# Rotating 96 images by 90 degrees: the last load in four strided pieces, and the first store gated by the first of them

## The chip, the cores and the metric

The kernel runs on one core of one Trainium2 chip. The metric is device time in microseconds (us) of the whole program, the median of several executions. A profile of one execution goes with it; its times count from the first instruction of the span.

## The reference

The input is 32 x 3 images of 256 x 256 float32 values, and each is turned clockwise by a quarter:

```python
def setup_inputs():
    batch, c, h, w = 32, 3, 256, 256
    return {"x": np.random.randn(batch, c, h, w).astype(np.float32)}

def reference(x: np.ndarray) -> np.ndarray:
    return np.rot90(x, k=-1, axes=(-2, -1)).astype(np.float32)
```

The output value at row r, column c of an image is the input value at row 255 - c, column r. No arithmetic is done. 25.17 MB are read from HBM, 25.17 MB are written.

## The kernel before

The 96 images are cut into 12 slabs of 8 images, 2 MB each. Each slab has an SBUF tile of its own (`units[0]` to `units[11]`, 128 partitions x 2 halves x 2048 values, so 8 KB for each partition and half); there is also one such tile in PSUM, `turned0`. `last` is 11.

**Loads** (lines 61 to 68). All 24 loads, two of 1 MB for each slab, are issued by SyncE (SP) in the order of the slabs. A middle slab (1 to 10) is loaded with 16 rows of an image to a partition: its first half goes to the even partitions, its second half to the odd ones, 64 partitions with 16 KB each (line 66). The first and the last slab are loaded with 8 rows to a partition: half i goes to all 128 partitions, 8 KB each (line 64). One contiguous run is one packet of the DMA, so packets are of 16 KB for the middle slabs and of 8 KB for the other two. `mark` (line 68) remembers the load of the first half of the last slab.

**Turning** (lines 70 to 82). VectorE (DVE) transposes blocks of 32 x 32 values; the access patterns of source and destination put the blocks where the rotation wants them. Each slab takes two instructions. The result of slab n is written into the tile of slab n - 1, which has been read by then; that of slab 0 goes to PSUM.

**Stores** (lines 84 to 97). They are issued by SP too, behind all loads, in packets of 8 KB. Slab 1 is stored first, in two halves of 1 MB (lines 85 and 88). A dependency written out by hand makes the first of these wait until `mark` has landed, "stores after loads". Slabs 2 and 11 are stored in two halves as well (line 91), slabs 3 to 10 with 2 MB each (line 93). Last comes slab 0: ScalarE (ACT) copies each half from PSUM into the tile of the last slab (line 96), free by then, and each half is stored (line 97).

Three things order the work around the change. SP issues its DMAs strictly in the program's order and waits, at each, for all that this DMA depends on; what is behind it waits too. The DMAs' completions are counted on eight semaphores in rotation, so a DMA also waits until the one eight places earlier has landed, which keeps at most eight loads in flight. And all DMAs go through one queue, spread over the 16 DMA engines; each DMA ends with one small completion packet on each engine.

Of the kernel before, what the change touches and what calls it, by code (L numbers as in the profile page):

```python
# [1 line left out]

# [4 lines left out]

@with_exitstack
def kernel(
    ctx: ExitStack,
    tc: tile.TileContext,
    x: bass.AP,
    out: bass.AP,
):

    nc = tc.nc
    fp32 = mybir.dt.float32

    B, C, H, W = x.shape  # L40
    P = nc.NUM_PARTITIONS
    RI, RO = 16, 8
    K = H // RI
    I = 2
    Q = P // (K * I)
    n_slabs = B * C // (Q * I)
    last = n_slabs - 1
    F = RO * W

    rows_in = x.rearrange("b c h w -> (b c h) w")  # L50
    rows_out = out.rearrange("b c h w -> (b c h) w")
    ld8_v = rows_in.rearrange("(n i p r) w -> n p i (r w)", i=I, p=P, r=RO)
    ld16_v = rows_in.rearrange("(n i m r) w -> n i m (r w)", i=I, m=Q * K, r=RI)
    st_v = rows_out.rearrange("(n i p c) w -> n p i (c w)", i=I, p=P, c=RO)

    pools = [ctx.enter_context(tc.tile_pool(name=f"unit{u}", bufs=1)) for u in range(n_slabs)]
    units = [pool.tile([P, I, F], fp32, name=f"u{u}") for u, pool in enumerate(pools)]
    psum = ctx.enter_context(tc.tile_pool(name="psum", bufs=1, space=bass.MemoryType.PSUM))
    turned0 = psum.tile([P, I, F], fp32, name="turned0")

    for n in range(n_slabs):
        for i in range(I):
            if n in (0, last):
                ld = nc.sync.dma_start(out=units[n][:, i], in_=ld8_v[n][:, i])  # L64
            else:
                ld = nc.sync.dma_start(out=units[n][i::I].rearrange("p i f -> p (i f)"), in_=ld16_v[n, i])  # L66
            if (n, i) == (last, 0):
                mark = ld

    for n in range(n_slabs):  # L70
        t_in, t_out = units[n], units[n - 1] if n else turned0
        if n in (0, last):
            for i in range(I):
                src = t_in[:, i].rearrange("p (r g c) -> p c r g", r=RO, c=RO)
                dst = t_out[:, i].rearrange("p (c g r) -> p c r g", c=RO, r=RO)
                nc.vector.transpose(out=dst[:, :, ::-1, ::-1], in_=src)  # L76
        else:
            src = t_in.rearrange("p i f -> p (i f)").rearrange("p (r g c) -> p c r g", r=RI, c=RO)
            dst = t_out.rearrange("p i (c k r) -> p c r k i", c=RO, r=RI)[:, :, ::-1, ::-1, :]
            for h in range(2):  # L80
                cs = slice(h * RO // 2, (h + 1) * RO // 2)
                nc.vector.transpose(out=dst[:, cs], in_=src[:, cs])  # L82

        if n == 1:
            first = nc.sync.dma_start(out=st_v[n][:, 0], in_=t_out[:, 0])  # L85
            tc.add_manual_dep(first.ins, mark.ins.name, mybir.DependencyInfo(
                mybir.DependencyClass.Sync, mybir.DependencyReason.SCHED_ONLY), reason="stores after loads")
            nc.sync.dma_start(out=st_v[n][:, 1], in_=t_out[:, 1])
        elif n in (2, last):
            for i in range(I):  # L90
                nc.sync.dma_start(out=st_v[n][:, i], in_=t_out[:, i])
        elif n:
            nc.sync.dma_start(out=st_v[n], in_=t_out)

    for i in range(I):
        nc.scalar.copy(out=units[last][:, i], in_=turned0[:, i])  # L96
        nc.sync.dma_start(out=st_v[0][:, i], in_=units[last][:, i])


# [1 line left out]
_INS = ['x']  # L101
_OUTS = [((32, 3, 256, 256), 'float32')]


# [23 lines left out]
```

## Time and profile before

| | |
|---|---|
| three runs | 123.69, 124.05, 124.07 us; median 124.05 |
| the profiled execution | 124.07 us, of which the span from first to last instruction is 122.3 |
| DVE busy | 93.3 us (76%), 24 instructions |
| ACT busy | 5.0 us (4%), 3 instructions |
| DMA | 50.33 MB in 5504 packets, mean 412 GB/s over the span |
| packets under 512 B | 640: 40 DMAs x 16 engines, the completions |
| loads | 24 of 1 MB, median 19.6 us from issue to landing |
| stores | 8 of 2 MB, median 22.0 us; 8 of 1 MB, median 13.7 us |

DVE works without a pause from 5.7 us to 99.4 us, one slab in 7.8 us. The stores begin near 60 us, when DVE has turned half of the slabs, and DVE stays ahead of them to the end. A DMA's time from issue to landing is mostly time in the queue behind others. The rows of SP that bear a line number show when it issued a DMA; they say nothing of when the data moved.

### The profile page before, as it was taken

The numbers are of one execution on the slowest core, as the hardware profiler recorded it, in microseconds if no ns is written. First come the engines' busy times: TensorE is split into PE (matmuls) and PEld (weight loads), VectorE is DVE, ScalarE is ACT, GpSimd is POOL, SyncE is SP. The second block draws the span as 40 slices with busy tenths as digits, with TensorE's granted clock in tenths as the row PEclk, the third lists the DMA queues.
The fourth block names the chain that finished last, engine by engine and source line by source line (L and its number), as shares of the span: only waits on it lengthen the run. The fifth ranks groups of instructions, "written<-read, shape, count | busy, mean of one in ns | idle before, by whom it ended". The sixth has DMA issues, their size and how long they took to land.

```text
span 122.3 us, 138 instructions
## 1 busy us (share of the span) xinstructions
DVE 93.3 (76%) x24; ACT 5.0 (4%) x3; POOL 0.2 (0%) x4
## 2 busy tenths in 40 slices
DVE  0199999999999999999999999999999950000000
ACT  0000000000000000000400000000000641000000
POOL 0000000000000000000000000000000000000000
DMA  3999999999999999999999999999999999999994
GB/s 86 426 431 429 434 429 434 439 429 439 423 429 429 429 429 429 429 429 405 423 423 429 429 426 429 429 426 418 423 429 415 418 421 426 426 421 415 418 421 193
DMA packets 5504, 50.33 MB, mean 412 GB/s; under 512 B 640, under 2 KB 640, under 8 KB 640
## 3 DMA queue, kind: packets, MB, share of 16 engines
q1 hardware_dynamic: 5504, 50.33, 97.9%
HBM read 25.17 MB, written 25.17 MB: 412 GB/s over the span
## 4 chain that ended last, share of the span: by engine, by line
DMA 49%; DVE 16%; issue 10%; DVEq 3%; SPq 3%; ACT 2%
DMA u<-in_x_dram 45%; DVE u L82 13%; DMA out_dram<-u 4%; DVE u L76 3%; DVEq L123 3%; SPq L66 2%; ACT u L96 2%; SPq L64 1%; SPq L85 0%
## 5 line engine op out<-in xcount | busy, mean ns | idle before, releaser
L82 DVE STREAM_TRANSPOSE u<-u 128x2048 f32<-128x2048 f32 x20 | 78.0, 3945 | 0.3
L76 DVE STREAM_TRANSPOSE turned<-u 128x2048 f32<-128x2048 f32 x2 | 7.6, 3828 | 5.7 <-DMA u<-in_x_dram 5.7
L76 DVE STREAM_TRANSPOSE u<-u 128x2048 f32<-128x2048 f32 x2 | 7.7, 3953 | 0.0
L96 ACT COPY u<-turned 128x2048 f32<-128x2048 f32 x2 | 3.7, 1866 | 36.6 <-DVE u L76 36.6
L96 ACT ACT_TABLE_LOAD x1 | 1.3, 1283 | 59.6 <-DMA u<-in_x_dram 59.6
L112 POOL MEMSET const-bfloat16-1.0<- 128x1 bf16 x1 | 0.1, 102 | 0.0
L112 POOL MEMSET const-uint8-127<- 128x1 uint8 x1 | 0.1, 101 | 0.0
L112 POOL MEMSET const-float32-0.0<- 128x1 f32 x1 | 0.1, 99 | 0.2 <-issue 0.2
L112 POOL MEMSET const-float32-1.0<- 128x1 f32 x1 | 0.1, 98 | 0.0
## 6 DMA issues: line engine op xcount, KB each, us to landing
u<-in_x_dram SPq DMA_DIRECT2D x24, 1024.0 KB, 19.6
out_dram<-u SPq DMA_DIRECT2D x8, 2048.0 KB, 22.0
out_dram<-u SPq DMA_DIRECT2D x8, 1024.0 KB, 13.7
```

What stands on the lines that cost most here:

```text
L64: ld = nc.sync.dma_start(out=units[n][:, i], in_=ld8_v[n][:, i])
L66: ld = nc.sync.dma_start(out=units[n][i::I].rearrange("p i f -> p (i f)"), in_=ld16_v[n, i])
L76: nc.vector.transpose(out=dst[:, :, ::-1, ::-1], in_=src)
L82: nc.vector.transpose(out=dst[:, cs], in_=src[:, cs])
L96: nc.scalar.copy(out=units[last][:, i], in_=turned0[:, i])
L112: nc = _bacc.Bacc("TRN2", target_bir_lowering=False, num_devices=1)
L123: with _tile.TileContext(nc) as tc:
```

## The change

The load of the second half of the last slab, 1 MB into 128 partitions, is split into four DMAs by partition: every eighth partition from 0 (16 partitions, 128 KB), every eighth from 4 (16), every fourth from 2 (32), and the odd ones (64). They are issued in this order. `mark` is now the first of them, instead of the load of the first half of that slab; the first store waits for it. Slabs 2 and 11 are stored by one DMA of 2 MB each, as the slabs between them, and so is slab 0, after both of ACT's copies. The program has 27 loads and 13 stores where it had 24 and 16. Nothing else is touched; DVE's and ACT's instructions are the same in the same order.

```diff
     for n in range(n_slabs):
         for i in range(I):
-            if n in (0, last):
-                ld = nc.sync.dma_start(out=units[n][:, i], in_=ld8_v[n][:, i])
+            if n == last and i:
+                parts = [slice(0, P, 8), slice(4, P, 8), slice(2, P, 4), slice(1, P, 2)]
+                mark = [nc.sync.dma_start(out=units[n][ps, i], in_=ld8_v[n][ps, i]) for ps in parts][0]
+            elif n in (0, last):
+                nc.sync.dma_start(out=units[n][:, i], in_=ld8_v[n][:, i])
             else:
-                ld = nc.sync.dma_start(out=units[n][i::I].rearrange("p i f -> p (i f)"), in_=ld16_v[n, i])
-            if (n, i) == (last, 0):
-                mark = ld
+                nc.sync.dma_start(out=units[n][i::I].rearrange("p i f -> p (i f)"), in_=ld16_v[n, i])
...
             nc.sync.dma_start(out=st_v[n][:, 1], in_=t_out[:, 1])
-        elif n in (2, last):
-            for i in range(I):
-                nc.sync.dma_start(out=st_v[n][:, i], in_=t_out[:, i])
         elif n:
             nc.sync.dma_start(out=st_v[n], in_=t_out)
 
     for i in range(I):
         nc.scalar.copy(out=units[last][:, i], in_=turned0[:, i])
-        nc.sync.dma_start(out=st_v[0][:, i], in_=units[last][:, i])
+    nc.sync.dma_start(out=st_v[0], in_=units[last])
```

## The prediction

> **What bounds the kernel now.** I read the page's slices first, then the DMA queue, then SP's waits, then the stretch around the change. In the page, the first line is the busy share of the 16 DMA engines in 40 slices of 3.06 us, the second what they moved, the third the queue's share of the span.
>
> ```profile
> DMA  3999999999999999999999999999999999999994
> GB/s 86 426 431 429 434 429 434 439 429 439 423 429 429 429 429 429 429 429 405 423 423 429 429 426 429 429 426 418 423 429 415 418 421 426 426 421 415 418 421 193
> q1 hardware_dynamic: 5504, 50.33, 97.9%
> ```
>
> The DMA engines are full from the second slice to the last but one. No compute engine can be the bound: what counts is how many bytes there are (unchanged), at what rate they move, and whether the stream ever runs dry. The switch from loads to stores lies near 61 us, at the border of slices 19 and 20 (423, 423 GB/s), and shows no hole. A closer look, in windows (stretch, its length, DVE, ACT, POOL busy, clock, DMA share, GB/s):
>
> ```profile
> 40.00:59.50 19.50, 19.43 (x6) 0.00 (x0) 0.00 (x0) 1.00 0.99 422
> 59.50:61.00 1.50, 1.47 (x2) 1.28 (x1) 0.00 (x0) 1.00 1.03 431
> 61.00:62.50 1.50, 1.50 (x1) 0.00 (x0) 0.00 (x0) 1.00 1.02 426
> 62.50:64.00 1.50, 1.50 (x1) 0.00 (x0) 0.00 (x0) 1.00 1.00 421
> 64.00:76.00 12.00, 11.93 (x5) 0.00 (x0) 0.00 (x0) 1.00 1.01 428
> 92.00:108.00 16.00, 7.37 (x2) 3.73 (x2) 0.00 (x0) 1.00 1.01 421
> 108.00:120.50 12.50, 0.00 (x0) 0.00 (x0) 0.00 (x0) 1.00 1.01 420
> ```
>
> The share stays at 1.00 or above through the switch (a packet counts in the window in which it starts, so a short window can pass 1). The present gate therefore loses nothing: no time is to be had there. SP's waits and issues around it (first who waits, us in total, times, longest; then the timeline's start, duration, instruction):
>
> ```profile
> SPq L66 <- DMA u<-in_x_dram: 25.8, 14, 2.0
> SPq L85 <- DMA u<-in_x_dram: 16.8, 1, 16.8
> ```
>
> ```profile
> 59.64 0.35 SPq L85 DMA_DIRECT2D out_dram<-u  x1
> 60.03 0.43 SPq L88 DMA_DIRECT2D out_dram<-u  x1
> 60.56 2.10 SPq L91 DMA_DIRECT2D out_dram<-u  x2
> ```
>
> SP sits 16.8 us at L85 until the first half of the last slab has landed (59.55), then issues the first store at 59.64. Loads go out eight deep and take 19.6 us each from issue to landing: 19.6 / 8 = 2.45 us per 1 MB. The last load, issued at 42.40, so lands at 62.0, and by the trace's packet records its last packets start between 60.9 and 61.2 on the 16 engines and end between 61.2 and 61.5, where store packets follow at once. A packet of 8 KB takes 0.309 to 0.32 us on its engine.
>
> **The change, part by part.**
>
> *The split load.* The last 1 MB load becomes pieces of 16, 16, 32 and 64 partitions, 128, 128, 256 and 512 KB: 1, 1, 2 and 4 packets of 8 KB for each engine, if each piece is spread over all 16. Bytes and packet size stay. Each piece ends with one completion packet per engine; those take 0.007 to 0.009 us in the records. Three more pieces: 3 x 0.009 = 0.03 us on the load side. SP's three more issues (0.33 us for an issue of this line, less or equal for a piece) go out when older loads land, at 42.4, 44.8, 47.3 and 49.7 by the present rhythm, inside SP's wait of 16.8 us and 10 us before the data's turn; without that cover they would cost 3 x 0.33 = 1.0 us.
>
> *The merged stores.* Slabs 2, 11 (last) and 0 go out as 2 MB instead of twice 1 MB. That saves three issues and three completion packets per engine, 0.03 us, which pays for the pieces: 40 DMAs before and after. Late stores of either form move alike by the landing records (4.98 us per 2 MB as one, 2.52 + 2.46 as two), so: 0. The last slab's store now waits for both transposes, 99.4 instead of 95.6, and slab 0's for both copies, 101.3. Today the store issued at 99.4 lands at 116.5, because 17 us of stores stand ahead of it; an unhindered 1 MB lands in 4.9, and the second half adds 2.5. Cover: 17.1 - 4.9 - 2.5 = 9.7 us. Nothing queued behind them on SP but each other and the end. DVE and ACT get a few more semaphore waits at 91.6 and 99.4 (17 to 28 ns each), under the same cover.
>
> *The moved gate, the one part on the path.* The gate opens when the first piece has landed: one packet per engine later, 2.45 / 8 = 0.31 us. The first store is issued at 59.64 + 0.31 = 59.95 instead of 59.64, and the two after it move along (the second is needed 2.45 us after the first, so it has room). What stands in the queue at that time shrinks from 2.45 us of loads to 7/8 of it, 2.14. Everything hangs on whether a store issued at 59.95 still comes in time. I bound it by two rows, DMA from issue to landing, first for the loads of L64, then for the store of L85:
>
> ```profile
> DMA to landing us min/median/max: 4.9/13.3/19.6
> ```
>
> ```profile
> DMA to landing us min/median/max: 4.9/4.9/4.9
> ```
>
> The minimum of the first is the kernel's first load, into empty queues: issued 0.72, landed 5.66 by the landing records, 4.94 us. The store took 59.64 to 64.50, 4.86 us, and landed 2.48 us after the last load: the stream, not its own start, set that time. So the present gate is within 0.1 us of what an unhindered 1 MB transfer needs. The upper bound: if the store needs the same 4.94 us, it lands at 59.95 + 4.94 = 64.89 against 64.50, a hole of **0.39 us**. The lower bound is **0**: the store reads SBUF where the first load read HBM, and its engines are already running, so its first bytes can be quicker by more than 0.39; nothing in the trace shows how much. The first packets of the first load start 1.05 to 1.83 us after its issue, at different times on different engines; the stores would be needed 1.25 to 1.6 us after theirs (61.2 to 61.55 less 59.95). That is the midst of the range, so I take the middle, **0.2 us**. A gain below 0 is excluded for this part, since the stream has no hole there.
>
> The sum: 124.07 (the profiled execution: 122.3 us of span and 1.8 around it) + 0.03 - 0.03 + 0 + 0.2 = 124.27, and, as that execution is 0.02 above the median of 124.05, **124.25 us**.
>
> [...]
>
> **The rivals.**
>
> *A: the full hole.* The store needs the 4.94 us of the first load. For it: the engines get their first descriptors over 0.8 us there, and the stream cannot hide it. Against: the load's HBM read is in it. 124.05 + 0.39 = 124.44. It decides from 4.92 us on (0.37 us of hole).
>
> *B, the one that ends clearly slower: the small pieces run under the full rate.* Place: the last 1 MB of loads. With one packet per piece and engine, in partitions 8 apart, engines could meet at the same part of SBUF, or completions could come too close together (0.31 us, where 2.45 is the closest in the trace). Price: if the first two pieces run at half rate, 2 x 0.31 = 0.62, 124.7; it decides from 0.37 us, the 1 MB taking 2.84 instead of 2.47. Against: the 64-partition loads also go to every second partition and run at 0.611 us per 16 KB, full rate. It would show the same if a piece were not spread over 16 engines, in which case the gate is not an eighth at all. [...]
>
> *C: hidden anyway.* The store starts quickly enough: 124.05.
>
> *D: faster.* Stores run at 428 GB/s from 64 to 76 us and at 420 to 421 after 92; their packets go from 0.309 to 0.314 us. If the other order of stores kept the first rate to the end, the 18.7 MB from 76 us on would take 43.7 instead of 44.4 us: -0.7, 123.35. For it: only that the rate is seen to differ. Against: it fell among 2 MB stores and did not come back with the 1 MB stores at the end.
>
> **How the numbers follow.** A difference under 0.3% (0.37 us) is about what a measurement of this kernel can tell from no change; the three runs lie 0.38 apart. Forecast (hole of 0 to 0.36) 0.53, C 0.07: within 0.3%, 0.60. A 0.15 and B 0.15: slower, 0.30. D 0.10: faster. The likeliest is 124.25. The range: down to 123.6, which leaves out most of D (0.08), up to 124.9, past A and B's price with the scatter of a run, leaving out some 0.05 where B reaches more pieces.
>
> **What would show it.** SP's wait at the first store's line ends at 59.9 and its issue starts near 59.95; the DMA share of 61.0 to 62.5 us falls from 1.02 to about 0.9 (0.2 / 1.5 = 0.13); the first store lands 4.7 to 4.9 us after issue. A landing 4.5 us after issue, with the share still at 1, is C; 4.9 with a hole is A. If the gate opens at 60.2 or later, or the last load lands past 62.2, it is B. A late store rate of 428 GB/s is D. I am wrong in kind if the time moves while the stretch from 59 to 65 us looks as before.

## The result, and the profile after

The changed kernel takes 124.75 us (median of 6 runs, which lie between 124.34 and 124.90), the kernel before 123.91 in the same session: ratio 1.0063, 95% interval 1.0045 to 1.0080. It is slower by 0.84 us, twice what a measurement can tell from no change. The profiled execution took 124.90 us with a span of 123.1, 0.83 above that of before. Each of the two profiles is that of the slowest execution of its six.

What the DMA engines moved in 40 slices (here of 3.08 us):

```profile
DMA  3999999999999999999999999999999999999995
GB/s 125 413 442 426 426 426 426 426 437 437 405 426 426 442 431 453 452 426 389 333 415 426 423 407 426 426 423 410 423 421 410 426 423 413 421 423 418 415 426 216
q1 hardware_dynamic: 5504, 50.33, 98.0%
```

The engines are as busy as before, but the 19th and 20th slices (55.4 to 61.6 us) move 389 and 333 GB/s where they moved 405 and 423. Busy engines that move less: packets take longer (8 KB in mostly 0.46 to 0.53 us in the first two pieces, where the kernel before takes 0.309 to 0.32). The windows around the switch (columns as in the prediction) say where:

```profile
59.50:61.00 1.50, 1.47 (x2) 0.89 (x1) 0.00 (x0) 1.00 0.94 317
61.00:62.50 1.50, 1.50 (x1) 0.39 (x1) 0.00 (x0) 1.00 1.01 421
62.50:64.00 1.50, 1.50 (x1) 0.00 (x0) 0.00 (x0) 1.00 0.97 399
64.00:76.00 12.00, 11.97 (x4) 0.00 (x0) 0.00 (x0) 1.00 1.01 423
92.00:108.00 16.00, 7.53 (x2) 3.73 (x2) 0.00 (x0) 1.00 1.01 420
108.00:120.50 12.50, 0.00 (x0) 0.00 (x0) 0.00 (x0) 1.00 1.01 420
```

Two things differ. From 59.5 to 61.0, before the switch, 317 GB/s move instead of 431: that is the split load. And the stores run at 423 GB/s from 64 to 76 us, where they had 428. SP's wait and issues of the first stores:

```profile
SPq L86 <- DMA u<-in_x_dram: 10.3, 1, 10.3
```

```profile
60.69 0.35 SPq L86 DMA_DIRECT2D out_dram<-u  x1
61.09 0.43 SPq L89 DMA_DIRECT2D out_dram<-u  x1
61.62 2.22 SPq L91 DMA_DIRECT2D out_dram<-u  x2
```

The first store goes out at 60.69, not at 59.95: the gate opened late too. The packet records complete the account. In the first two pieces an 8 KB packet takes mostly 0.46 to 0.53 us, in the third about 0.43 and then 0.35, in the fourth 0.31 again. (The records do not name the DMA or the engine; this is read from their times.) Each piece is spread over all 16 engines: every one has 16 landings, those of the first between 59.44 and 60.59 us. Landings, averaged over the 16 engines: the loads end at 62.29 instead of 61.79 (+0.50), the stores then take 59.80 instead of 59.32 us (+0.48), and the slowest engine is 0.2 behind the mean at the end instead of 0.35 (-0.15). Together +0.83 for this execution. The engines stand idle between loads and stores for 0.04 us on average, so there is hardly a hole.

Part of the gate's lateness belongs to this execution: one load's landing on the first and on the last engine lay 0.80 us apart, 0.39 before, and the gate waited for the last (the first piece's at 60.59, the issue at 60.69). In another kernel with the same gate and the same sets of partitions in SBUF (runs in HBM alone, below) the store went out at 60.34.

### The profile page after: what moved, and what is told of

Read it like the earlier page. It is cut to its first block, busy times and chain, and to the rows that moved or that the text cites. A ratio compares the mean times of both kernels' runs of the same rounds, so it can differ in the third digit from the quotient of the medians.

```text
span 123.1 us, 139 instructions
## 1 busy us (share of the span) xinstructions
DVE 93.5 (76%) x24; ACT 5.0 (4%) x3; POOL 0.2 (0%) x4
## 4 chain that ended last, share of the span: by engine, by line
DVE 46%; issue 27%; DMA 4%; DVEq 3%; ACT 2%
DVE u L83 37%; DVE turned L77 6%; DMA u<-in_x_dram 4%; DVE u L77 3%; DVEq L121 3%; ACT u L94 2%; DVEq L77 0%
```

## The experiments

The working theory after the result: the strided pieces run below the full rate (S), because of where they lie (P) or because they are short (S2). Against it the hole in front of the first store (H) and the merged stores (M). Ratios are to the kernel before, run beside each kernel on the same chip. Lead means the mean landing of the last load less the issue of the first store; the time of the stores runs from that mean landing to the mean end.

**Parts of the change alone.** The split with the old gate and stores:

```diff
+            if n == last and i:
+                parts = [slice(0, P, 8), slice(4, P, 8), slice(2, P, 4), slice(1, P, 2)]
+                for ps in parts:
+                    nc.sync.dma_start(out=units[n][ps, i], in_=ld8_v[n][ps, i])
```

> The last 1 MB load in the four strided pieces of the change; the gate stays at the landing of the slab's first half, and the stores are those of before. Theory S (the pieces themselves run below the full rate, because of which partitions they hold): packets of the first three pieces take 0.35 to 0.5 us instead of 0.31, the loads end 0.5 to 0.6 us later, ratio 1.004 to 1.005. Rival H (the later gate leaves a hole in front of the first store): no hole is made here, ratio 0.999 to 1.001. Rival M (the merged stores are slower): ratio 0.999 to 1.001.

Measured 1.0037 (1.0025 to 1.0049), just under what S expected. Its loads end at 62.28 on average, 0.49 later than before, and its stores then run at the old pace:

```profile
59.50:61.00 1.50, 1.47 (x2) 1.14 (x1) 0.00 (x0) 1.00 1.02 350
61.00:62.50 1.50, 1.50 (x1) 0.15 (x1) 0.00 (x0) 1.00 0.97 404
64.00:76.00 12.00, 11.93 (x5) 0.00 (x0) 0.00 (x0) 1.00 1.01 427
```

350 GB/s in the first window, 427 in the last: the split alone costs the half microsecond of the loads, and nothing after them.

The merge alone (the three pairs of 1 MB stores as 2 MB each):

> Only the stores of slabs 2, 11 and 0 merged into 2 MB each; loads and gate as before. Theory S: nothing, ratio 0.999 to 1.001. Rival M: the store stretch is slower from the start (423 GB/s instead of 428 from 64 to 76 us), ratio 1.001 to 1.003. Rival H: nothing.

Measured 1.0011 (1.0001 to 1.0021), some 0.1 us, at the edge of what can be seen. The ratio lies in M's range, but M's sign is not there: the stores ran at 427 GB/s from 64 to 76 us, and the stretch was 59.27 us. Where the 0.1 us went stays open.

Split and merge, with the old gate:

> The change without its later gate: strided pieces and merged stores, the first store again gated by the slab's first half. If the gate's move costs nothing of its own, this is as slow as the change, ratio 1.005 to 1.007. If the move costs the rest of the sum of the parts (1.0063 less 1.0037 of the split and 1.0011 of the merge), 1.0045 to 1.005.

Measured 1.0042 (1.0026 to 1.0057), so the move of the gate has about 0.002 of the 1.0063, some 0.26 us, by itself, though the two intervals overlap. Its stores took 59.24 us, 0.56 less than those of the change: one profile each puts the gate's share at twice what the ratios do.

**Where the pieces' slowness comes from.** First, pieces cut along the row of each partition, 128 partitions in each:

```diff
-                parts = [slice(0, P, 8), slice(4, P, 8), slice(2, P, 4), slice(1, P, 2)]
-                mark = [nc.sync.dma_start(out=units[n][ps, i], in_=ld8_v[n][ps, i]) for ps in parts][0]
+                parts = [slice(0, F // 8), slice(F // 8, F // 4), slice(F // 4, F // 2), slice(F // 2, F)]
+                mark = [nc.sync.dma_start(out=units[n][:, i, fs], in_=ld8_v[n][:, i, fs]) for fs in parts][0]
```

> The changed kernel with its last 1 MB load cut along the 8 KB of each partition (1, 1, 2 and 4 KB from all 128 partitions) instead of by partitions; gate on the first piece, an eighth again, stores merged, as many pieces and completions as in the changed kernel. Theory S: without the sparse sets of partitions the loads run at the full rate but for the shorter packets of 1 and 2 KB; the gate opens by 60.0 us and the ratio to the kernel before is 1.000 to 1.003. Rival S2 (it is four completions close together that cost, not the partitions): loads end 0.5 us late here too, ratio 1.004 to 1.007. Rival H: the hole stays, up to 0.39 us, ratio up to 1.003 with load packets at full rate.

Measured 1.0117 (1.0090 to 1.0145): a miss for both. The short packets had a trouble of their own: in the first piece some 1 KB packets took up to 0.5 us and engines stood idle (0.2 us on average). What can still be read: the pieces then landed at 61.26, 61.60, 62.24 and 63.49, that is 0.34, 0.64 and 1.25 us for 128, 256 and 512 KB, nearly the full rate with completions 0.34 us apart. Completions that close together did not cost here, which speaks against S2. Each of these pieces has eight packets for each engine, though; whether a piece of one packet for each engine is slow by its shortness alone, wherever it lies, no run tested.

Then the sets of partitions themselves, on either side of the transfer: runs of neighbours in SBUF and in HBM, in HBM alone, in SBUF alone.

```diff
...
-                mark = [nc.sync.dma_start(out=units[n][ps, i], in_=ld8_v[n][ps, i]) for ps in parts][0]
+                strided = [slice(0, P, 8), slice(4, P, 8), slice(2, P, 4), slice(1, P, 2)]
+                runs = [slice(0, 16), slice(16, 32), slice(32, 64), slice(64, P)]
+                mark = [nc.sync.dma_start(out=units[n][ps, i], in_=ld8_v[n][hs, i]) for ps, hs in zip(runs, runs)][0]
```

> The changed kernel with its four pieces cut as runs of neighbouring partitions (0 to 15, 16 to 31, 32 to 63, 64 to 127) instead of strided sets; sizes, count, gate and stores as in the change. Theory P (the strided sets are slow, in HBM or SBUF): full rate, ratio to the kernel before about 1.001 to 1.002. Rival S2 (short pieces with their completions close together are slow, whatever they hold): packets of 0.35 to 0.5 us as in the change, ratio 1.005 to 1.008. Rival Q (16 neighbouring partitions share few ways into SBUF): slower than the change, packets of 0.6 us and more in the first pieces, ratio above 1.008.

> As the change in SBUF (strided sets of partitions), but each piece reads a run of neighbouring 8 KB rows of HBM, so the last 1 MB is put into the wrong partitions and half a slab of the output is permuted. If the HBM side of the strided pieces is slow: full rate, ratio 1.001 to 1.002. If the SBUF side or the shortness of the pieces is: as the change, 1.005 to 1.008.

> The reverse: pieces go to runs of neighbouring partitions but read the strided rows of HBM of the change (the same half slab of the output is permuted in another way). If the HBM side is slow: as the change, 1.005 to 1.008. If the strided SBUF side is: 1.001 to 1.002. If neighbouring partitions share few ways into SBUF: as the kernel with runs on both sides, whatever that is.

| last 1 MB: SBUF side | HBM side | ratio |
|---|---|---|
| strided (the change) | strided | 1.0063 (1.0045 to 1.0080) |
| strided | runs | 1.0057 (1.0042 to 1.0071) |
| runs | strided | 1.0246 (1.0221 to 1.0271) |
| runs | runs | 1.0233 (1.0215 to 1.0251) |

The HBM side makes no difference that can be seen; with the pieces' sizes kept, the SBUF side takes the loss from 0.6% to 2.3% or more. Windows of the kernel before, and below it of the kernel with runs on both sides:

```profile
58.50:61.50 3.00, 2.96 (x2) 1.28 (x1) 0.00 (x0) 1.00 0.99 410
61.50:64.00 2.50, 2.50 (x1) 0.00 (x0) 0.00 (x0) 1.00 1.03 436
66.00:76.00 10.00, 9.93 (x4) 0.00 (x0) 0.00 (x0) 1.00 1.01 428
76.00:92.00 16.00, 15.93 (x5) 0.00 (x0) 0.00 (x0) 1.00 1.01 423
108.00:119.00 11.00, 0.00 (x0) 0.00 (x0) 0.00 (x0) 1.00 1.01 419
```

```profile
58.50:61.50 3.00, 2.96 (x2) 0.47 (x1) 0.00 (x0) 1.00 1.16 183
61.50:64.00 2.50, 2.50 (x1) 0.81 (x1) 0.00 (x0) 1.00 0.93 200
76.00:92.00 16.00, 15.93 (x5) 0.00 (x0) 0.00 (x0) 1.00 1.01 429
108.00:119.00 11.00, 0.00 (x0) 0.00 (x0) 0.00 (x0) 1.00 1.01 427
```

In the first two rows of the latter the engines are busy and move less than half the rate. Packets take up to 1.2 us, mostly 0.9 to 1.2, while the pieces of 16 and 32 neighbours run, and about 0.6 in that of 64. In the change every eighth partition took 0.46 to 0.53, every fourth 0.43 and then 0.35, and the odd ones 0.31. What rival Q expected came (a ratio above 1.008, packets of 0.6 us and more); the few shared ways that it names were the author's conjecture, and no run shows them. Why a set is slow stays open, for the neighbours as for the strided pieces. The runs show that which partitions a piece holds in SBUF decides how much is lost, and how much that is.

The last two rows were not expected: after so slow a load, the stores run at 427 to 429 GB/s to the end, where the kernel before falls to 419.

**What the gate costs.** To see how fast a store starts, the gate was put on the whole last load:

```diff
-            if (n, i) == (last, 0):
+            if (n, i) == (last, 1):
```

> The kernel before with the gate moved to the landing of the whole last load: SP issues the first store near 62.1 us, into empty queues. It measures what a store needs from issue to landing when nothing stands before it, the quantity that the prediction had to bound. By the first load's row, 4.94 us: the first store lands at 67.05 instead of 64.50, ratio 1.0205 (+2.55 us). If the store starts quicker, by 0.4 us say: 4.54, landing at 66.65, ratio 1.017.

Measured 1.0033 (1.0017 to 1.0049). It did not test what it was made for: in the program as built the second store, which had no gate, went first, at 44.9 us, and queued behind the loads; the gated one followed at 62.10. So all stores of slabs 1 to 11 were given the dependency:

> The kernel before with all stores of slabs 1 to 11 held until the whole last load has landed; in the kernel with the gate on the last load alone, SP had issued the second store at 44.9 us, ahead of the gated one, so that no hole could form. Now the first store is issued near 62.1 us into empty queues. It measures what a store needs from issue to landing with nothing before it. By the first load's row, 4.94 us: landing at 67.05 instead of 64.50, ratio 1.0205. If it starts 0.4 us quicker: 66.65, ratio 1.017.

Measured 1.0184 (1.0165 to 1.0203). The first store's issue, and the hole:

```profile
62.17 0.82 SPq L85 DMA_DIRECT2D out_dram<-u  x2
```

```profile
60.50:61.25 0.75, 0.75 (x1) 0.47 (x1) 0.00 (x0) 1.00 0.86 360
61.25:62.00 0.75, 0.75 (x1) 0.00 (x0) 0.00 (x0) 1.00 0.04 11
62.00:62.75 0.75, 0.75 (x1) 0.00 (x0) 0.00 (x0) 1.00 0.00 0
62.75:63.50 0.75, 0.75 (x1) 0.00 (x0) 0.00 (x0) 1.00 0.84 350
66.00:76.00 10.00, 9.93 (x4) 0.00 (x0) 0.00 (x0) 1.00 1.00 410
```

Its first packets start 0.85 to 1.0 us after the issue, on all engines within 0.15 us, and it lands after 3.91 us. The first load into empty queues needs 4.94, with first packets after 1.05 to 1.83 us. So here a store into empty queues had to be issued 0.85 to 1.0 us ahead of its turn, and H is refuted as a hole. Its landing, 1.6 us later than before, is less than the 2.3 us that this kernel loses: the last row shows where most of the rest went, in stores that run at 410 GB/s behind the hole instead of 428.

The gate's move without any split: a GpSimd copy stands between the landing and the store.

```diff
...
+    spare = spare_pool.tile([P, 64], fp32, name="spare")
...
-                mark = ld
+                mark = nc.gpsimd.tensor_copy(out=spare[:, :], in_=units[n][:, i, :64])
```

> The kernel before, loads and stores as they were, but the first store now waits for a GpSimd copy of 64 columns of the slab's first half into a spare tile, which waits for the landing of that half: the store goes out some 0.2 to 0.4 us later than before, near 59.9, with the last load in one piece. With all stores held until the loads had landed, the first packets started 0.85 to 1.0 us after the issue; the loads end at 61.2 to 61.5. Theory (the move of the gate by itself is hidden): no hole, ratio 0.999 to 1.001. Rival H (a store that late leaves a hole): 0.2 to 0.4 us, ratio 1.0015 to 1.003.

> The same with 512 columns: the store goes out some 0.6 to 1.2 us later than before. With 0.85 to 1.0 us from issue to first packets, holes begin when the issue is later than 60.3 and grow one for one: an issue at 60.5 costs 0.1 to 0.3 us (1.001 to 1.002), one at 60.8 0.4 to 0.6 us (1.003 to 1.005). If nothing is lost even there, the start of a queued store is quicker than that of one in empty queues.

With 64 columns the store went out at 59.80 (0.16 later than before): 1.0029 (1.0019 to 1.0039). With 512 columns at 60.21 (0.57 later): 1.0045 (1.0033 to 1.0057). Neither has a hole (engines idle for 0.01 us), and both are slower than a gate whose move is hidden; the first lies in H's range, but without H's hole. In the second, the stores are slow from the start:

```profile
61.50:64.00 2.50, 2.50 (x1) 0.00 (x0) 0.00 (x0) 1.00 1.01 423
66.00:76.00 10.00, 9.93 (x4) 0.00 (x0) 0.00 (x0) 1.00 1.01 417
76.00:92.00 16.00, 15.93 (x5) 0.00 (x0) 0.00 (x0) 1.00 1.01 419
```

417 GB/s from 66 to 76 us, where the kernel before has 428; packets take 0.317 us on average there instead of 0.310. This is the other part of the change's loss, without pieces and without a hole. What the added copy itself may cost was not measured apart; the profiled execution of the first of the two, at 124.02 us, is the fastest of its seven (median 124.28), so its profile shows little of its 0.3%.

Across the kernels, from one profile each:

| kernel | lead, us | stores, us |
|---|---|---|
| pieces along the row | 1.46 | 59.98 |
| late gate, 512 columns | 1.55 | 59.83 |
| the change | 1.60 | 59.80 |
| late gate, 64 columns | 1.98 | 59.43 |
| runs in HBM alone | 1.99 | 59.45 |
| before | 2.15 | 59.32 |
| merge alone | 2.21 | 59.27 |
| split and merge | 2.37 | 59.24 |
| split alone | 2.39 | 59.17 |
| runs in SBUF alone | 2.98 | 58.63 |
| runs on both sides | 3.92 | 58.44 |

In this table, the earlier the stores are queued ahead of the loads' landing, the faster they run. Two kernels are not in it. That with all stores held has a lead of -0.36 and a hole. That with the gate on the last load alone does not fit: its first store had a lead of 17.0 us, the others were issued from 62.10 on, and its stores took 59.42 us. So one early store is not enough. Even so, the table asked for the gate to be moved the other way.

```diff
-            if (n, i) == (last, 0):
+            if (n, i) == (last - 1, 1):
```

> The kernel before with the first store gated one step earlier, by the landing of the last load of slab 10 (near 57.1 us), so that it is issued 4.6 us before the loads have landed instead of 2.2. In the kernels so far the store stretch, from the mean landing of the loads to the mean end, was shorter the earlier the first store had been issued: 59.8 us at a lead of 1.6 us, 59.4 at 2.0, 59.3 at 2.2, 59.2 at 2.4, and 58.4 to 58.6 at 3.0 to 3.9 (the latter with pieces that also pushed the engines apart). Theory L (the lead itself sets the pace of the stores): 58.5, ratio 0.993 to 0.995, faster than both kernels. Theory F (a late issue disturbs how the engines stand to each other, an early enough one changes nothing, and it was the pushing apart that made the store packets take 0.309 us to the end): as the kernel before, ratio 0.999 to 1.001.

Measured 0.9978 (0.9967 to 0.9989): 123.70 us against 124.06 for the kernel before in that session, so faster than that kernel and, by the ratios, than the change.

```profile
58.50:61.50 3.00, 2.96 (x2) 1.28 (x1) 0.00 (x0) 1.00 0.94 374
61.50:64.00 2.50, 2.50 (x1) 0.00 (x0) 0.00 (x0) 1.00 1.04 439
66.00:76.00 10.00, 9.93 (x4) 0.00 (x0) 0.00 (x0) 1.00 1.02 430
76.00:92.00 16.00, 15.93 (x5) 0.00 (x0) 0.00 (x0) 1.00 1.01 427
108.00:119.00 11.00, 0.00 (x0) 0.00 (x0) 0.00 (x0) 1.00 1.01 429
```

The first row pays: with stores already queued, the last loads are disturbed (374 GB/s instead of 410, the DMA share 0.94 instead of 0.99) and end 0.27 us later on average, at 62.06. The other rows gain: store packets take 0.309 us in every stretch to the end, and the stores need 58.75 us, 0.57 less, with a lead of 4.90 us. Net -0.30 in the profiles, about what the ratio says. Theory L had the direction and left out what the loads lose; theory F, that nothing changes, falls. But F's other half is not refuted: at the switch the engines were pushed apart here too (one DMA's landings spread over 0.36 us before and 0.63 to 0.77 after). In the three kernels whose stores kept or nearly kept 0.309 us (this one and the two with runs in SBUF) that spread is 0.6 us or more during the stores; in most of the slow ones it is 0.3 to 0.55. But it is 0.8 to 0.9 in the kernel with pieces along the row, which has the slowest stores of the table, and grows to 1.1 in that with the gate on the last load: a wide spread is not enough either. Whether the lead acts by itself or by the distance it leaves between the engines or by something else stays open: the packet records do not name the engine.

## Why the prediction was right or wrong

The range, 123.6 to 124.9, holds 124.75; the likeliest case does not: it was "within 0.3%" at 124.25, and the change is slower by 0.63%. That the range held is in part luck. Its top was set by rivals A and B; B came, A did not, and a cost that stood in no term and in no rival took A's place. The kernel before was also quicker in that session (123.91) than the 124.05 that the range started from: 124.05 + 0.84 is 124.89.

- **What bounds the kernel** was right: the DMA stream alone (its engines are busy 97.9% of the span before, 98.0% after), and no hole to be closed at the old switch (DMA share 1.03 and 1.02 from 59.5 to 62.5 us).
- **"Bytes and packet size stay"**, taken to mean that the time of a packet stays, is the step that failed. It let the pieces run at 0.309 to 0.32 us a packet; they took 0.46 to 0.53 in the first two. The cost was in the text as rival B, with a guess at the cause (engines meeting at the same part of SBUF, which no run shows) and 0.62 us as its price; the loads ended 0.50 later. Both of B's signs came: the gate opened after 60.2, the last load landed after 62.2 (at 62.83). B had 0.15 of the chance; against it stood that "the 64-partition loads also go to every second partition and run at 0.611 us per 16 KB, full rate". That row does not carry over: it speaks for the fourth piece, the odd partitions, which ran at full rate (0.31 us per 8 KB) just as those loads do, and not for sets of partitions four or eight apart with one or two packets for each engine. Which of the two, the set or the few packets, makes the strided pieces slow was not separated.
- **The hole** of 0.2 us was mis-sized: 0.04 us. The bound of 4.94 us from the first load was too far off: a store into empty queues lands 3.91 us after its issue. Rival A is refuted, and of C the part is right that the start is hidden.
- **The gate's cost** nevertheless came, as the prediction did not foresee: not as idle time but as store packets that are up to 1.4% longer (0.314 us on average instead of 0.310 from 66 to 76 us; 59.80 us for all the stores instead of 59.32). The prediction looked for holes as the only cost of the gate: "A gain below 0 is excluded for this part, since the stream has no hole there". A full stream ran at two paces here (0.309 us a packet to the end with the early gate, 0.317 from 66 to 76 us with the late one of 512 columns); rival D had that, but only as a gain from the order of the stores. The early gate shows that a gain was to be had.
- **The time of the gate**, 59.95, was 60.69: slow pieces, and an execution with its engines further apart. An issue of a piece took SP 0.49 to 0.52 us, not 0.33 or less; inside SP's wait that cost nothing.
- **The merged stores at 0**: 1.0011, small, place unknown.
- **Rival D** had 0.10, with the 428 GB/s not coming back against it. The rate is real: 427 to 430 to the end in two of the kernels. But the order of the stores does not bring it (the merge alone has 419 to 421 after 92 us); moving the gate earlier did, and the change moves it later.

## What to carry to other kernels

When a load is cut by partition, ask which partitions each piece holds: here pieces with one packet for each engine lost about a third of their rate or more (every eighth partition: 0.46 to 0.53 us a packet instead of 0.31) or up to three quarters (16 neighbours: up to 1.2 us), whatever their HBM side (ratios 1.0063 and 1.0057, 1.0246 and 1.0233). A busy DMA row is not a row at full pace (here 317 GB/s at a share of 0.94, where the kernel before had 431 at 1.03): compare GB/s and packet times between stretches, since the loss here was in load packets of 0.46 us and store packets of 0.314 instead of 0.310 and not in gaps. When loads turn into stores on one queue, try the gate of the first stores earlier (here a lead of 4.9 us was better than 2.2, and 1.6 worse) and count what the last loads lose by it.

## What the runs showed of the hardware

- A store into empty queues starts moving 0.85 to 1.0 us after its issue and lands 3.91 us after it (1 MB); the first load of the program needs 4.94.
- Loads into runs of neighbouring partitions, 16 or 64 at a time, take 0.9 to 1.2 us and 0.6 us for an 8 KB packet instead of 0.31, with the engines shown busy (DMA share 1.16 and 0.93, at 183 and 200 GB/s); into every eighth partition 0.46 to 0.53.
- With the same loads and stores in the same order, and the engines busy during the stores (DMA share 1.01 to 1.04), 59 to 60 us of stores ran at different paces by when the first was issued: 0.309 us a packet to the end (lead 4.9 us), 0.310 rising to 0.315 (2.2), or 0.317 from 66 to 76 us and 0.315 after (1.6).
